# Split weights in seven one-operand tiles and raw weights in four buffers, in a fused convolution and attention layer

## The chip, the cores and the metric

The kernel runs on one core of a Trainium2 chip, in one launch. The metric is the device time of one execution in microseconds, taken as the median of several executions. A core has TensorE (PE in the profile, with its weight loads on a row of their own, PEld), VectorE (DVE), ScalarE (ACT), GpSimd (POOL) and SyncE (SP), which here issues nearly all loads. Each of them works through its instructions in the order that they have in the program.

## The reference

One layer over 512 latent tokens and 256 context tokens of width 1024, in float32. A combined projection `h @ w_in` (1024 x 10240) feeds a gated short convolution and a neighbourhood attention of 16 heads; the two are merged under sigmoid gates and go through a last projection `w_o`.

```python
parts = _split_in(h @ w_in[i])            # b, c, x, z_a, q, k, v, z_b, g_a, g_b, 1024 columns each
q = _apply_rope(_heads(parts[4]), cos, sin)
k = _apply_rope(_heads(parts[5]), cos, sin)
v = _heads(parts[6])
kv_c = hc @ w_in[i][:, K_OFF:V_END]       # keys and values of the context tokens
...
attn = _neighbourhood_attention(q, k, v, k_c, v_c, rpb[i])
y_a = (jax.nn.silu(z_a) * b_gate * _dwconv3(c_gate * x_in, conv_w, conv_b)) @ w_out_conv
y_b = (jax.nn.silu(z_b) * attn_o) @ w_out_attn
merged = jax.nn.sigmoid(g_a) * y_a + jax.nn.sigmoid(g_b) * y_b
y = merged @ w_o
x = x + gt[:, None, :] * _rmsnorm(y, post_g[i])
```

## The kernel before

**Numbers in two parts.** Every large product is done in a reduced-width float32 with each operand cut into a high part H and a low part L. `split` makes them: ACT casts the source to H (L67), then DVE subtracts H from the source and writes L (L70). A product is three matmuls (H·H, H·L, L·H). Weights are split on the fly, and so are the attention's probabilities, whose parts are called TH and TL.

**Chunks.** Weights come in chunks of 256 columns, 1 MB each, in an order that is a list in the program (L237 to L240). A chunk is two raw halves of 512 KB (tile `raw`, L87: three buffers, loaded by SP at L89), each with 512 of the 1024 rows. Split weights live in tiles `w` (L81: four buffers of 8 KB per partition). There are two kinds of chunk:

- An ordinary chunk (`Chunk.split`, L91) takes two `w` tiles, one per half, each with H and L of four row blocks. Two units of 24 matmuls use it (L164 to L166; value chunks go by L177 and L182).
- A paired chunk goes by a Strassen-like scheme with seven products of 12 matmuls (`pair`, L294, the matmuls at L289). `first` (L98) makes four operands, B11 and B21 in one `w` tile, the sums T1 and T2 in another. `second` (L114) makes T3 and T4 in a third and B22 (with B12 where the context needs it) in a fourth. ACT copies results from PSUM (L300 to L311) and DVE adds the others (L306, L314, L317). L306 reads a PSUM bank that the first product of the second half writes again, so that product waits for L306.

The calls of paired and ordinary chunks are interleaved with the attention of earlier heads: scores (PE L717 and L726, DVE L733, ACT L740, L744, L747), `turn2`, which transposes probabilities (PE L754) and splits them into TH and TL, and `gather` (PE L773), which multiplies them with V. After a gather, ACT copies (L778) and DVE adds and gates the result (L779, L780, L785, L786). All these share the instruction streams of ACT and DVE with the splits of the next chunk. Where each stands in its stream is settled when the program is built, by a scheduler that lays out instructions by its own estimates and by when buffers come free. SP's stream holds the raw loads and, between them, the bias loads `bt` (L709) and modulation weights `wm` (L369, L569).

**The end.** The last projection is again a Strassen scheme, on 512-column operands that `moving` (L931) splits: wB11, wB21, wT1, wT2, wT3, wT4, each in two `w` tiles.

Of the kernel before, what the change touches and what calls it, by code (L numbers as in the profile page):

```python
# [15 lines left out]
P = 128  # L16
# [11 lines left out]
def layer(ctx: ExitStack, tc, xp, ctxt, ctxT, cc, wmod, small, wfirst, win, wout, wo, rel, tab, out):  # L28
# [49 lines left out]


    def wtile(shape):  # L80
        return wp.tile(shape, F32R, name="w", bufs=4)  # L81

    class Chunk:


        def __init__(self, src):
            self.raws = [wp.tile([P, 4, 256], F32, name="raw", bufs=3) for _ in range(2)]  # L87
            for i, raw in enumerate(self.raws):
                nc.sync.dma_start(raw, src[:, 4 * i:4 * i + 4])  # L89

        def split(self):  # L91
            t = [wtile([P, 4, 2, 256]) for _ in range(2)]
            for x, raw in zip(t, self.raws):
                split(x[:, :, 0], x[:, :, 1], raw)
            k = range(KT)
            return tuple([t[i // 4][:, i % 4, y] for i in k] for y in range(2)) + ([t[i // 4][:, i % 4] for i in k],)

        def first(self, keep=False):  # L98
            (b11, b12), (b21, b22) = self.b = [(r[:, :, :P], r[:, :, P:]) for r in self.raws]
            t, sums = (wtile([P, 2, 2, 4, P]) for _ in range(2))  # L100
            split(t[:, 0, 0], t[:, 0, 1], b11)
            nc.vector.tensor_add(b11, b11, b12)
            split(sums[:, 0, 0], sums[:, 0, 1], b11)
            split(t[:, 1, 0], t[:, 1, 1], b21)
            nc.vector.tensor_add(b11, b11, b22)
            split(sums[:, 1, 0], sums[:, 1, 1], b11)
            self.keep = keep
            if not keep:
                nc.vector.tensor_add(b12, b12, b22)
            nc.vector.tensor_add(b21, b21, b11)  # L110
            self.B = {"B11": t[:, 0], "B21": t[:, 1], "T1": sums[:, 0], "T2": sums[:, 1]}
            return self

        def second(self):  # L114
            t, last = (wtile([P, 2, 2, 4, P]) for _ in range(2))
            (_, b12), (b21, b22) = self.b
            if self.keep:
                split(last[:, 1, 0], last[:, 1, 1], b12)
                nc.vector.tensor_add(b12, b12, b22)
            for n, x, b in (("T3", t[:, 0], b12), ("T4", t[:, 1], b21), ("B22", last[:, 0], b22)):  # L120
                split(x[:, 0], x[:, 1], b)
                self.B[n] = x
            self.B["B12"] = last[:, 1]


    behind = None
# [1 line left out]
    class Chunks:  # L128
# [13 lines left out]
        def ready(self, n):  # L142
            if n in self.raw:
                c, kind = self.raw.pop(n), self.srcs[n][1]
                self.ahead[n] = c.first(kind == "qk") if kind else c.split()

        def __call__(self):
            self.load(self.n)
# [82 lines left out]
        "cx": lambda j: win[2 * j], "bz": lambda j: win[2 * j + 1],  # L231
    }
    def paired(n, i):
        return n == "g" or n == "qk" and i in (3, 4, 6) or n == "zb" and i < 3 or n in ("cx", "bz") and i > 4

    order = [(win[i], False) for i in range(8)] + [(qk(0), False), (vz(0, 0), False)]
    order += [(where[n](i), n if paired(n, i) else False) for f in plan for n, i in f] + [(vz(3, 1), paired("zb", 3))]  # L237
    merge = ["g2", "g3", "y0", "g4", "y1", "g5", "y2", "g6", "y3", "g7", "y4", "y5", "y6", "y7"]
    order += [(win[32 + int(m[1])], paired("g", int(m[1]))) if m[0] == "g" else (wout[int(m[1])], False) for m in merge]
# [688 lines left out]
        for q in range(2):  # L928
            nc.vector.tensor_add(dst[q], x[q], y[q])

    def moving(src, dst=None):  # L931
        if dst is None:
            t = [wtile([P, 2, 2, S]) for _ in range(2)]
            dst = [[x[:, y] for x in t] for y in range(2)]
        for q in range(2):
            split(dst[0][q], dst[1][q], src[q])
        return dst
# [11 lines left out]
    for j in range(KT):  # L949
        w = chunk()  # L950
        g = [G[j][:, i] for i in range(2)]
        if j in (4, 6):
            raws[j // 2] = G[j]
        m2 = raws[j // 2][:, j % 2]
        for i in range(2):
            nc.vector.scalar_tensor_tensor(
                out=g[i], in0=g[i], scalar=1.0, in1=unit(w, i, ua[i]), op0=ALU.add, op1=ALU.mult
            )
            if j == 7 and i == 0:
                A2 = [bp.tile([P, 2, S], F32R, name=f"A2{k}", tag=f"us{k}") for k in range(4)]  # L960
                for k in range(3):
                    split(A2[k][:, 0], A2[k][:, 1], raws[2 + k // 2][:, k % 2])
        nc.vector.tensor_add(m2, g[0], g[1])
        if j < 4:
            for _ in merge_gates(j + 4):
                pass
        if j == 4:

            nc.vector.tensor_scalar(out=gains[:, 0:4], in0=gains[:, 0:4], scalar1=0.5, scalar2=None, op0=ALU.mult)
            nc.vector.tensor_scalar(out=gains[:, 4:8], in0=gains[:, 4:8], scalar1=-0.5, scalar2=None, op0=ALU.mult)  # L970
            gpost = bp.tile([P, D], F32, name="gpost")
            for i in range(2):
                gb = cv.tile([P, S], F32, name="ta")
                ps = pj()
                for k in range(4):
                    n = 4 * i + k
                    nc.vector.tensor_copy(gb[:, k * P:(k + 1) * P], gains[:, n:n + 1].broadcast_to([P, P]))
                    nc.tensor.transpose(ps[:, k * P:(k + 1) * P], gb[:, k * P:(k + 1) * P], ident)
                nc.scalar.copy(gpost[:, i * S:(i + 1) * S], ps)
        if j == 4:  # L980
            A11, S3 = operand("A11", hp, ("u2", "u3")), operand("S3", hp, ("a2", "a3"))
            for q in range(2):
                split(A11[q][:, 0], A11[q][:, 1], raws[q][:, :, h0])
                x = cv.tile([P, S], F32, name="tb").rearrange("p (k c) -> p k c", k=2)
                nc.vector.tensor_sub(x, raws[q][:, :, h0], raws[q][:, :, h1])
                split(S3[q][:, 0], S3[q][:, 1], x)
            B11, B12 = quarter("B11", hp, ("s0", "s1")), quarter("B12", hp, ("u0", "u1"))
            B22, B21, T2, T3 = (quarter(n, hp, (f"h{2 * i}", f"h{2 * i + 1}")) for i, n in enumerate(("B22", "B21", "T2", "T3")))
            for t, i in ((B11, (0, 0)), (B12, (0, 1)), (B22, (1, 1)), (B21, (1, 0))):
                load_block(t, *i)  # L990
        if j == 5:
            sums1(0)
        if j == 6:
            nc.scalar.activation(const.tile([P, 1], F32, name="dummy2"), G[7][:, 1, :1], AF.Sqrt, bias=eps, scale=0.0)
            wB11 = moving(B11)
            total(B11, B11, B12)
            T1 = B11
            total(T2, T1, B22)
            total(T3, B12, B22)
            T4 = B12  # L1000
            total(T4, T2, B21)
# [63 lines left out]
    sums1(1)  # L1065
    for q in range(2):
        split(X1[q][:, 0], X1[q][:, 1], raws[q][:, :, h1])
    wT1 = moving(T1)
    both(fb, a12, wB21, True)
    for q in range(2):  # L1070
        split(S2[q][:, 0], S2[q][:, 1], raws[q][:, :, h0])
# [12 lines left out]
        squares(t, c0, 0, added(P1s[:, t], fb[t]))  # L1084
        partial(t, 0, True)
    both(fa, stationary(S2), wT2, False, snap(U2s, fa))
    wT3 = moving(T3)

    def block12(t):
        squares(t, c1, 1, added(U2s[:, t], fe[t]))  # L1090
# [113 lines left out]
```

## Time and profile before

| | |
|---|---|
| median of 3 runs | 709.25 us (709.1 to 709.57) |
| profiled execution | 709.01 us, its span 707.2 us |
| busy | PE 695.0 us (98%), DVE 586.3 (83%), ACT 436.5 (62%), POOL 66.9 (9%) |
| chain that ended last | PE 91%, DVE 4%, DMA 2%, ACT 1% |
| TensorE clock granted | 1.00 in every stage |

The span is the time from the first to the last instruction in the profile; 1.8 us of the execution's time lie outside it. A row of the timeline gives start, duration, engine, line, operation, output and inputs, and how many like instructions it merges; in brackets stands how long the engine was idle before it, and what ended the wait. Durations on ACT and DVE overlap a little, so that the distance between two starts is shorter than a duration.

### The profile page before, as it was taken

The page shows a single profiled execution, that of the slowest core. Times are in us where ns is not written, and L with a number is a line of the kernel's source. Part 1 is how long each engine was busy: PE and PEld are TensorE (multiplying, and loading weights), DVE is VectorE, ACT ScalarE, POOL GpSimd, SP SyncE. Part 2 cuts the span into 40 slices and gives each one's busy share as a digit, 9 for nine tenths or more (in the row PEclk, how much of TensorE's full clock was granted, in tenths as well). Part 3 has the DMA queues.
Part 4 walks back from the last instruction along what each step waited for, and adds up shares of the span by engine and source line. Part 5 has one row for each costly group of instructions (what it writes and reads, how often), then busy time and mean ns, then how long its engine had stood idle before and what let it go on. Part 6 is the DMA issues. An engine that isn't in the chain of part 4 may idle for free.

```text
span 707.2 us, 11426 instructions
## 1 busy us (share of the span) xinstructions
PE 695.0 (98%) x4196; PEld 618.0 (87%) x4196; DVE 586.3 (83%) x1114; ACT 436.5 (62%) x868; POOL 66.9 (9%) x110
## 2 busy tenths in 40 slices
PE   7999999999999999999999999999999999999996
PEld 4888888888889989898999999999898899988885
DVE  6979997668599989978898797999799676665996
ACT  6566632656577677775876766778693444442563
POOL 0000002230130310301302203000000000000000
PEclk9999999999999999999999999999999999999998
DMA  8996896564351563542635436313733233560013
GB/s 338 406 354 227 284 339 173 131 164 144 99 105 24 135 176 116 127 138 60 168 106 165 103 125 157 101 61 105 247 117 116 87 120 120 198 250 30 31 59 120
DMA packets 37466, 108.27 MB, mean 153 GB/s; under 512 B 5025, under 2 KB 5281, under 8 KB 37410
## 3 DMA queue, kind: packets, MB, share of 16 engines
q1 hardware_dynamic: 28946, 92.20, 37.8%
q0 software_dynamic: 8320, 15.21, 10.7%
q8 instruction: 33, 0.54, 0.3%
q14 instruction: 23, 0.19, 0.1%
q10 hardware_dynamic: 144, 0.13, 0.1%
HBM read 87.07 MB, written 5.24 MB: 131 GB/s over the span
## 4 chain that ended last, share of the span: by engine, by line
PE 91%; DVE 4%; DMA 2%; ACT 1%; issue 1%; SPq 0%; POOL 0%; DVEq 0%; ACTq 0%
PE ps L289 25%; PE ps L164 11%; PE ps L166 11%; PE ps L165 11%; PE ps L177 6%; PE ps L1008 5%; PE ps L773 4%; PE ps L754 3%; PE ps L182 3%; PE ps L717 3%; PE ps L196 2%; PE ps L424 2%; PE ps L428 2%; PE ps L425 2%; DMA fraw<-in_wfirst 1%; PE ps L726 1%
## 5 line engine op out<-in xcount | busy, mean ns | idle before, releaser
L67 ACT CAST w<-raw 128x512 fp32r<-128x512 f32 (+1 forms) x193 | 137.3, 733 | 95.9 <-PE ps L166 31.3
L70 DVE TENSOR_TENSOR w<-raw,w 128x512 fp32r<-128x512 f32 (+1 forms) x193 | 156.6, 824 | 42.3 <-ACT w L67 40.9
L289 PE MATMUL ps<-S,w 128*128 128x256 f32 x960 | 121.9, 283 | 0.0
L289 PEld LDWEIGHTS ps<-S,w 128*128 128x128 f32 x960 | 118.2, 192 | 0.1
L289 PE MATMUL ps<-h,w 128*128 128x256 f32 x720 | 94.0, 284 | 0.6 <-DVE tc L306 0.5
L289 PEld LDWEIGHTS ps<-h,w 128*128 128x128 f32 x720 | 89.9, 191 | 2.5 <-DVE tc L306 0.7
L164 PE MATMUL ps<-h,w 128*128 128x512 f32 x208 | 81.5, 392 | 0.0
L166 PE MATMUL ps<-h,w 128*128 128x512 f32 x208 | 81.2, 390 | 0.0
L165 PE MATMUL ps<-h,w 128*128 128x512 f32 x208 | 81.0, 390 | 0.0
L626 POOL DMA_DIRECT2D tc<-tb x32 | 28.8, 1175 | 286.7 <-DVE tc L624 197.7
L747 ACT ACTIVATE pt<-pt,z 128x512 f32<-128x512 f32 x64 | 43.0, 724 | 6.0 <-DVE z L745 5.9
L166 PEld LDWEIGHTS ps<-h,w 128*128 128x128 f32 x208 | 39.0, 188 | 8.3
L165 PEld LDWEIGHTS ps<-h,w 128*128 128x128 f32 x208 | 39.1, 188 | 8.0
L164 PEld LDWEIGHTS ps<-h,w 128*128 128x128 f32 x208 | 39.1, 188 | 7.9
L67 ACT CAST TH<-ps 128x512 fp32r<-128x512 f32 x64 | 35.8, 589 | 15.5 <-PE ps L754 15.5
L733 DVE CUSTOM_DVE_ANT_1 ps<-ps,bt 128x512 f32<-128x512 f32 x56 | 38.8, 693 | 6.8 <-PE ps L717 6.5
L70 DVE TENSOR_TENSOR TL<-ps,TH 128x512 fp32r<-128x512 f32 x64 | 42.2, 682 | 1.0 <-ACT TH L67 0.7
L754 PE MATMUL ps<-ident,pt 128*128 128x128 f32 x256 | 33.3, 273 | 0.0
L177 PE MATMUL ps<-w,h 128*128 128x512 f32 x128 | 32.3, 394 | 0.0
L754 PEld LDWEIGHTS ps<-ident,pt 128*128 128x128 f32 x256 | 29.2, 140 | 2.1 <-ACT pt L747 0.2
L740 ACT ACTIVATE pt<-ps,m 128x512 f32<-128x512 f32 x32 | 22.0, 688 | 12.5 <-DVE m L733 11.8
L773 PE MATMUL ps<-TH,V 128*128 128x256 f32 (+1 forms) x96 | 28.5, 319 | 0.2 <-ACT TH L67 0.2
(249 smaller groups left out, 1387.8 us busy)
## 6 DMA issues: line engine op xcount, KB each, us to landing
raw<-in_win SPq DMA_DIRECT2D x74, 512.0 KB, 4.4
wm<-in_wmod SPq DMA_DIRECT2D x34, 512.0 KB, 6.4
raw<-in_wout SPq DMA_DIRECT2D x16, 512.0 KB, 3.6
bt<-in_rel SPq DMA_DIRECT2D x16, 256.0 KB, 2.9
tc<-tb POOLq DMA_DIRECT2D x32, 128.0 KB, 3.6
B<-in_wo SPq DMA_DIRECT2D x8, 512.0 KB, 6.4
fraw<-in_wfirst SPq DMA_DIRECT2D x8, 384.0 KB, 8.6
qd<-qd POOLq DMA_DIRECT2D x24, 128.0 KB, 2.3
```

Source lines behind the costliest of these rows:

```text
L67: cast = nc.scalar.copy(H, src)
L70: nc.vector.tensor_sub(L, src, H.bitcast(F32))
L164: nc.tensor.matmul(ps, lhsT=H[k][:, cs], rhs=mH[k], start=k == 0, stop=False)
L165: nc.tensor.matmul(ps, lhsT=H[k][:, cs], rhs=mL[k], start=False, stop=False)
L166: nc.tensor.matmul(ps, lhsT=L[k][:, cs], rhs=mH[k], start=False, stop=k == KT - 1)
L177: nc.tensor.matmul(ps, lhsT=mH[k][:, ts], rhs=both[k].rearrange("p a c -> p (a c)"), start=k == 0, stop=False, skip_group_check=True,)
L289: nc.tensor.matmul(ps, lhsT=w[:, x, k], rhs=act[y][k], start=start and k + o == 0, stop=k == 3 and o == 2, skip_group_check=True,)
L733: nc.vector.tensor_tensor_reduce(out=s3, in0=s3, in1=bt[:, e::4 - e][:, 0:2], scale=-1.0, scalar=3.0e38, op0=ALU.add, op1=ALU.min, accum_o ...
L747: nc.scalar.mul(x, x, z[:, i:i + 1])
L754: nc.tensor.transpose(tp[:, c], pt[:, c * P:(c + 1) * P], ident)
L773: nc.tensor.matmul(o3[:, dst], lhsT=V[p][:, kt, h], rhs=src(t), start=n == 0 and t is TH, stop=n == len(work) - 1 and t is TL,)
L1008: nc.tensor.matmul(out, lhsT=a(x, k, ts), rhs=w[y][k // 2][:, k % 2, cols], start=start and k + o == 0, stop=k == 3 and o == 2, skip_group ...
```

## The change

The raw weights get a fourth buffer, so two whole chunks fit. The split weights get seven tiles of 4 KB per partition, one operand each: one of the Strassen operands (H and L side by side), or H alone or L alone of half an ordinary chunk. The four value chunks, whose matmuls want H and L side by side, take four tiles with a quarter of the chunk's rows each (`beside`), so they are split in four pairs of 128x512 instructions and not in two of 128x1024. The value chunks are marked "v" in the list for that, and `ready` sends them to `split`. In the last projection wB11, wT1 and wT3 go into the four raw buffers (`spare`), the others into four `w` tiles. Together both pools hold as much as before: 4·8 + 3·4 = 44 KB per partition, and now 7·4 + 4·4 = 44 KB. No matmul is added or removed. Below line 125 a line of the changed kernel has a number higher by 7 (10 from L940 on) than before.

```diff
     def wtile(shape):
-        return wp.tile(shape, F32R, name="w", bufs=4)
+        return wp.tile(shape, F32R, name="w", bufs=7)
...
-            self.raws = [wp.tile([P, 4, 256], F32, name="raw", bufs=3) for _ in range(2)]
+            self.raws = [wp.tile([P, 4, 256], F32, name="raw", bufs=4) for _ in range(2)]
...
-        def split(self):
-            t = [wtile([P, 4, 2, 256]) for _ in range(2)]
-            for x, raw in zip(t, self.raws):
-                split(x[:, :, 0], x[:, :, 1], raw)
+        def split(self, beside=False):
+
             k = range(KT)
-            return tuple([t[i // 4][:, i % 4, y] for i in k] for y in range(2)) + ([t[i // 4][:, i % 4] for i in k],)
+            if beside:
+                t = [wtile([P, 2, 2, 256]) for _ in range(4)]
+                for i, x in enumerate(t):
+                    split(x[:, :, 0], x[:, :, 1], self.raws[i // 2][:, 2 * (i % 2):2 * (i % 2) + 2])
+                return tuple([t[i // 2][:, i % 2, y] for i in k] for y in range(2)) + ([t[i // 2][:, i % 2] for i in k],)
+            t = []
+            for raw in self.raws:
+                t.append([wtile([P, 4, 256]) for _ in range(2)])
+                split(*t[-1], raw)
+            return tuple([t[i // 4][y][:, i % 4] for i in k] for y in range(2)) + (None,)
+
+        def operand(self, name, b):
+            x = self.B[name] = wtile([P, 2, 4, P])
+            split(x[:, 0], x[:, 1], b)
 
         def first(self, keep=False):
...
-            t, sums = (wtile([P, 2, 2, 4, P]) for _ in range(2))
-            split(t[:, 0, 0], t[:, 0, 1], b11)
+            self.B = {}
+            self.operand("B11", b11)
             nc.vector.tensor_add(b11, b11, b12)
-            split(sums[:, 0, 0], sums[:, 0, 1], b11)
-            split(t[:, 1, 0], t[:, 1, 1], b21)
+            self.operand("T1", b11)
+            self.operand("B21", b21)
             nc.vector.tensor_add(b11, b11, b22)
-            split(sums[:, 1, 0], sums[:, 1, 1], b11)
+            self.operand("T2", b11)
...
         def second(self):
...
-            for n, x, b in (("T3", t[:, 0], b12), ("T4", t[:, 1], b21), ("B22", last[:, 0], b22)):
-                split(x[:, 0], x[:, 1], b)
-                self.B[n] = x
+            for n, b in (("T3", b12), ("T4", b21), ("B22", b22)):
+                self.operand(n, b)
...
-                self.ahead[n] = c.first(kind == "qk") if kind else c.split()
+                self.ahead[n] = c.first(kind == "qk") if kind and kind != "v" else c.split(kind == "v")
...
-    def moving(src, dst=None):
+    def moving(src, dst=None, spare=False):
         if dst is None:
-            t = [wtile([P, 2, 2, S]) for _ in range(2)]
-            dst = [[x[:, y] for x in t] for y in range(2)]
+            if spare:
+                t = [wp.tile([P, 2, S], F32R, name="wr", tag="raw", bufs=4) for _ in range(4)]
+            else:
+                t = [wtile([P, 2, S]) for _ in range(4)]
+            dst = t[::2], t[1::2]
...
-            wB11 = moving(B11)
+            wB11 = moving(B11, spare=True)
...
-    wT1 = moving(T1)
+    wT1 = moving(T1, spare=True)
...
-    wT3 = moving(T3)
+    wT3 = moving(T3, spare=True)
```

The change also moves instructions. Three places are shown, of the kernel before and then of the changed one. The paired chunk in them is the convolution's chunk cx 5; its raw halves are raw_2547 and raw_2548 before and raw_2586 and raw_2587 after.

SP's loads up to that chunk and the next, before:

```order
L89 DMA raw_2313<-in_win 128x1024
L709 DMA bt_1039<-in_rel 128x512 x2
L89 DMA raw_2314<-in_win 128x1024
L89 DMA raw_2547<-in_win 128x1024
L709 DMA bt_1039<-in_rel 128x512
L89 DMA raw_2548<-in_win 128x1024
L89 DMA raw_2736<-in_win 128x1024
```

and in the change:

```order
L89 DMA raw_2349<-in_win 128x1024
L283 DMA usc4_98<-ta_1743 128x512
L716 DMA bt_1051<-in_rel 128x512
L89 DMA raw_2350<-in_win 128x1024
L716 DMA bt_1051<-in_rel 128x512
L89 DMA raw_2586<-in_win 128x1024
L89 DMA raw_2587<-in_win 128x1024
L716 DMA bt_1051<-in_rel 128x512
L89 DMA raw_2778<-in_win 128x1024
```

The two halves of the chunk now stand next to each other, ahead of the bias load that stood between them. Before, the second half goes into the buffer of raw_2313, the first half of the chunk just ahead of it; now it goes into that of raw_2004, the last half of the chunk before that one.

ACT's stream around the gather that comes next, before (L67 with TH is the split of transposed probabilities, L303, L305 copies of results, L744 an exponential):

```order
L67 CAST w_2575<-raw_2547 128x512
L303 COPY tc_2483<-ps_2494 128x256
L305 COPY tc_2483<-ps_2492 128x256
L67 CAST w_2575<-raw_2548 128x512
L67 CAST TH_2342<-ps_2561 128x512
L744 ACTIVATE pt_2556,z_2470<-ps_2551,m_2554 128x512
L67 CAST TH_2342<-ps_2562 128x512
L67 CAST w_2576<-raw_2547 128x512
```

and in the change:

```order
L310 COPY tc_2521<-ps_2533 128x256
L312 COPY tc_2521<-ps_2531 128x256
L67 CAST TH_2378<-ps_2600 128x512
L67 CAST TH_2378<-ps_2601 128x512
L751 ACTIVATE pt_2595,z_2508<-ps_2590,m_2593 128x512
L754 ACTIVATE pt_2507<-pt_2507,z_2508 128x512
L754 ACTIVATE pt_2595<-pt_2595,z_2508 128x512
L67 CAST w_2618<-raw_2586 128x512
L67 CAST w_2621<-raw_2587 128x512
```

The cast from the chunk's second raw half (raw_2548, raw_2587) stood ahead of both TH casts and stands behind them now, and so do the subtractions that follow on DVE.

DVE's stream ahead of the add L306 of that chunk (L313 in the change), before (tb and at are the gate and the attention's result, kl a key's low part, L733 the score's bias and minimum):

```order
L779 TENSOR_TENSOR at2_2643<-ps_2644,ta_2657 64x448
L785 SCALAR_TENSOR_TENSOR tb_2629<-tb_2629,tc_2482 128x512
L785 SCALAR_TENSOR_TENSOR tb_2633<-tb_2633,tc_2483 128x512
L786 SCALAR_TENSOR_TENSOR at0_1589<-at0_1589,tb_2629 128x512
L786 SCALAR_TENSOR_TENSOR at0_1589<-at0_1589,tb_2633 128x512
L70 TENSOR_TENSOR kl_2440<-tc_2257,ks_2438 128x512
L780 TENSOR_TENSOR at2_2643<-ps_2644,ta_2657 64x64
L733 ISA ps_2661,m_2664<-ps_2661,bt_1039 128x512
L733 ISA m_2664 128x1
L70 TENSOR_TENSOR w_2673<-raw_2548,w_2673 128x512
L70 TENSOR_TENSOR w_2674<-raw_2548,w_2674 128x512
L306 TENSOR_TENSOR tc_2671<-tc_2671,ps_2682 128x256
```

and in the change:

```order
L787 TENSOR_TENSOR at2_2684<-ps_2685,ta_2698 64x64
L740 ISA ps_2702,m_2705<-ps_2702,bt_1051 128x512
L740 ISA m_2705 128x1
L792 SCALAR_TENSOR_TENSOR tb_2670<-tb_2670,tc_2520 128x512
L792 SCALAR_TENSOR_TENSOR tb_2674<-tb_2674,tc_2521 128x512
L793 SCALAR_TENSOR_TENSOR at0_1613<-at0_1613,tb_2670 128x512
L793 SCALAR_TENSOR_TENSOR at0_1613<-at0_1613,tb_2674 128x512
L70 TENSOR_TENSOR kl_2478<-tc_2293,ks_2476 128x512
L70 TENSOR_TENSOR w_2714<-raw_2586,w_2714 128x512
L70 TENSOR_TENSOR w_2717<-raw_2587,w_2717 128x512
L70 TENSOR_TENSOR w_2720<-raw_2587,w_2720 128x512
L313 TENSOR_TENSOR tc_2712<-tc_2712,ps_2724 128x256
```

All three subtractions of the chunk's second half now stand between the gate and the add, where two of them stood before (the first, from raw_2547, stood ahead of L779).

More of the change, by code (lines that the diff above doesn't have):

```diff
@@ L110, in first @@
             nc.vector.tensor_add(b21, b21, b11)
-            self.B = {"B11": t[:, 0], "B21": t[:, 1], "T1": sums[:, 0], "T2": sums[:, 1]}
             return self
         def second(self):
-            t, last = (wtile([P, 2, 2, 4, P]) for _ in range(2))
             (_, b12), (b21, b22) = self.b
             if self.keep:
-                split(last[:, 1, 0], last[:, 1, 1], b12)
+                self.operand("B12", b12)
                 nc.vector.tensor_add(b12, b12, b22)
-            for n, x, b in (("T3", t[:, 0], b12), ("T4", t[:, 1], b21), ("B22", last[:, 0], b22)):
-                split(x[:, 0], x[:, 1], b)
-                self.B[n] = x
-            self.B["B12"] = last[:, 1]
+            for n, b in (("T3", b12), ("T4", b21), ("B22", b22)):
+                self.operand(n, b)
     behind = None
@@ L233, in paired @@
     def paired(n, i):
-        return n == "g" or n == "qk" and i in (3, 4, 6) or n == "zb" and i < 3 or n in ("cx", "bz") and i > 4
-    order = [(win[i], False) for i in range(8)] + [(qk(0), False), (vz(0, 0), False)]
+        return n == "v" or n == "g" or n == "qk" and i in (3, 4, 6) or n == "zb" and i < 3 or n in ("cx", "bz") and i > 4
+    order = [(win[i], False) for i in range(8)] + [(qk(0), False), (vz(0, 0), "v")]
     order += [(where[n](i), n if paired(n, i) else False) for f in plan for n, i in f] + [(vz(3, 1), paired("zb", 3))]
```

## The prediction

> **What bounds the kernel now.** I read the shares of the page first, then the chain of waits.
>
> ```profile
> PE 695.0 (98%) x4196; PEld 618.0 (87%) x4196; DVE 586.3 (83%) x1114; ACT 436.5 (62%) x868; POOL 66.9 (9%) x110
> PE 91%; DVE 4%; DMA 2%; ACT 1%; issue 1%; SPq 0%; POOL 0%; DVEq 0%; ACTq 0%
> ```
>
> TensorE is the bound, and no matmul changes. The change can give no more than the time in which TensorE stands still behind a split, a load or something queued behind these. The busy time by stretches of 20 us (columns: PE, PEld, DVE, ACT, POOL, each with its count, then clock, DMA share, GB/s) is 20.00 for PE in all stretches from 20 to 700 us but two:
>
> ```profile
> 220.00:240.00 20.00, 20.00 (x149) 18.93 (x148) 18.88 (x43) 16.04 (x38) 0.00 (x0) 1.00 0.19 56
> 240.00:260.00 20.00, 19.38 (x151) 18.43 (x150) 17.52 (x37) 14.77 (x32) 7.20 (x11) 1.00 0.61 152
> 260.00:280.00 20.00, 19.44 (x153) 18.51 (x152) 19.03 (x41) 14.89 (x33) 1.03 (x2) 1.00 0.41 133
> ```
>
> The waits of TensorE name who ended them (us in total, times, longest); the others lie in the first 20 us, before any chunk:
>
> ```profile
> PE ps L289 <- DVE tc L306: 0.5, 1, 0.5
> PE ps L773 <- DVE TL L70: 0.5, 1, 0.5
> PE ps L773 <- ACT TH L67: 0.2, 1, 0.2
> ```
>
> A busy row of PE overlaps the next one, so a stall costs more than the idle time shown. I take it from distances between starts on PE's timeline:
>
> ```profile
> 247.04 1.04 PE L754 MATMUL ps<-ident,pt 128*128 128x128 f32 x8
> 247.84 1.68 PE L289 MATMUL ps<-h,w 128*128 128x256 f32 x12
> 249.35 3.04 PE L289 MATMUL ps<-S,w 128*128 128x256 f32 x24
> 252.55 0.49 PE L773 MATMUL ps<-TH,V 128*128 128x512 f32 x1 [0.16 <-ACT TH L67]
> 253.50 0.50 PE L773 MATMUL ps<-TL,V 128*128 128x512 f32 x1 [0.45 <-DVE TL L70]
> 253.83 0.40 PE L773 MATMUL ps<-TH,V 128*128 128x512 f32 x1
> 254.07 0.39 PE L773 MATMUL ps<-TL,V 128*128 128x512 f32 x1
> ...
> 261.93 1.03 PE L754 MATMUL ps<-ident,pt 128*128 128x128 f32 x8
> 263.44 1.69 PE L289 MATMUL ps<-h,w 128*128 128x256 f32 x12 [0.47 <-DVE tc L306]
> ...
> 269.57 3.46 PE L289 MATMUL ps<-h,w 128*128 128x256 f32 x24
> ```
>
> *First stall, the gather at 252.55.* The 24 matmuls ahead of it stand 0.12 apart and should hand over at 249.35 + 24·0.12 = 252.23: 0.32 us late. From its TH to its TL go 0.95 us where the next pair needs 0.24 (253.83 to 254.07): 0.71. The next start is another 0.09 late. Together 1.12. *Second, the product at 263.44.* Eight transposes take 0.80 us up to the next start at 247.04, and 1.51 at 261.93: 0.71. *Third, inside 269.57.* 24 matmuls take 3.46 where those at 249.35 take 3.04; 0.08 of the 0.42 is the usual slow first one (1.68 for the 12 at 247.84, which at 0.12 would make 1.60), so 0.34. Sum: 2.17 us. That is the whole prize between 20 and 700 us.
>
> Why is the first gather late? Its splits stand behind the chunk's second raw half, on ACT and on DVE, and that half came late:
>
> ```profile
> 228.50 0.89 SPq L89 DMA_DIRECT2D raw<-in_win  x2
> 238.58 0.33 SPq L709 DMA_DIRECT2D bt<-in_rel  x1
> 244.39 2.38 SPq L89 DMA_DIRECT2D raw<-in_win  x2
> ```
>
> ```profile
> 250.24 0.62 ACT L67 CAST w<-raw 128x512 fp32r<-128x512 f32 x1 [3.08 <-DMA raw<-in_win]
> 250.76 0.58 ACT L67 CAST TH<-ps 128x512 fp32r<-128x512 f32 x1
> 251.91 0.59 ACT L67 CAST TH<-ps 128x512 fp32r<-128x512 f32 x1
> ```
>
> ```profile
> 243.64 1.29 DVE L70 TENSOR_TENSOR w<-raw,w 128x512 fp32r<-128x512 f32 x2
> 250.89 0.69 DVE L70 TENSOR_TENSOR w<-raw,w 128x512 fp32r<-128x512 f32 x1 [2.19 <-ACT w L67]
> ...
> 258.02 1.28 DVE L785 SCALAR_TENSOR_TENSOR tb<-tb,tc 128x512 f32<-128x512 f32 x2
> 259.23 1.28 DVE L786 SCALAR_TENSOR_TENSOR at<-at,tb 128x512 f32<-128x512 f32 x2
> 260.43 0.68 DVE L70 TENSOR_TENSOR kl<-tc,ks 128x512 fp32r<-128x512 f32 x1
> 261.77 1.28 DVE L70 TENSOR_TENSOR w<-raw,w 128x512 fp32r<-128x512 f32 x2
> 262.98 0.41 DVE L306 TENSOR_TENSOR tc<-tc,ps 128x256 f32<-128x256 f32 x1
> 270.86 0.41 DVE L317 TENSOR_TENSOR tc<-tc,ps 128x256 f32<-128x256 f32 x1
> ```
>
> With three raw buffers the half raw_2548 has to wait for the last split from raw_2313, done at about 244.3; it is issued at 244.39, and ACT waits 3.08 us for it with both TH casts queued behind.
>
> **The change part by part.** *Fourth raw buffer.* By the order shown, raw_2587 goes into the buffer of raw_2004, a value chunk's half, and stands behind no bias load any more. The pair at 228.50 shows when SP is free for it, and that chunk has been split by then; so it lands some 15 us earlier, into a stretch whose DMA share is 0.19. The bias load that was issued at 238.58 now stands behind it and is not held up. The scheduler has also put both TH casts ahead of that half's split. From the first TH cast to the end of TL there are four instructions on two engines and no wait for a load; the transposes they read end by 248.1 (247.04 + 1.04), so with DVE's distances of 0.60 (1.29 less 0.69 in the row of 243.64) TL is done at about 249.6, 2.6 us ahead of the 252.23 at which it is wanted. First stall: -1.12. If the load were late after all: 0.
>
> *Second stall, same price.* The product waits for L306, which waits for DVE's own stream: 258.02 to 263.39 is unbroken work of 0.60 a piece. In the changed order three, not two, subtractions of the chunk stand between gate and add (+0.60), but the work ahead of the gate starts earlier, as DVE no longer idles 2.19 us. What decides is when the gate can start: the gather's result is ready 1.12 earlier, ACT copies it behind two more casts, and I put L779 at about 255.5. Then follow L779 and L780 (0.67), L733 (0.60), four gate instructions (2.40), kl (0.60), three subtractions (1.80), L306 (0.41): 262.0, and 0.25 for small gaps, 262.25. TensorE wants it at 261.93 + 0.80 - 1.12 = 261.61. So about 0.64 us of the 0.71 stays. Bounds: 0 if L306 profits by the 2.19 us in full; 1.23 if DVE moves up only with the gather (263.39 - 1.12 + 0.60 against 261.61).
>
> *Third stall.* L317 at 270.86 ends 0.34 too late for its product, with a queue of sums and splits of the next chunk ahead. Its splits no longer share a tile, so they are spread; I walk B21 of that chunk to 268.3, wanted at 269.8, and take -0.34. Bounds: 0 and -0.34.
>
> *Seven one-operand tiles.* A tile comes free with its one operand, so splits of the next paired chunk can begin piece by piece. Ordinary chunks get less: two of them used all four tiles, and now the eighth piece, L of the second half, must wait until the first piece of the chunk before is read out. This shows in waits that are there already:
>
> ```profile
> ACT w L67 <- PE ps L166: 44.6, 20, 7.1
> ```
>
> ```profile
> 85.66 0.39 PE L165 MATMUL ps<-h,w 128*128 128x512 f32 x1
> ...
> 98.35 0.39 PE L164 MATMUL ps<-h,w 128*128 128x512 f32 x1
> ```
>
> Such a chunk runs 2·24 matmuls, 0.2266 apart (56 steps from the first row to the last), 10.9 us. Its first piece is last read after 36 of them, at 8.2; the next chunk's eighth piece is wanted at its fifth row block, 10.9 + 12·0.2266 = 13.6. That leaves 5.4 us for one subtraction of 1.2. No cost taken; the bounds are in the third rival.
>
> *Value chunks in quarters.* Eight casts and eight subtractions more. By the rows
>
> ```profile
> 254.39 1.16 ACT L67 CAST w<-raw 128x512 fp32r<-128x512 f32 x2
> 44.74 2.00 ACT L67 CAST w<-raw 128x1024 fp32r<-128x1024 f32 x2
> 45.83 2.36 DVE L70 TENSOR_TENSOR w<-raw,w 128x1024 fp32r<-128x1024 f32 x2 [0.27 <-ACT w L67]
> ```
>
> and the one at 243.64, starts stand 0.52 and 0.96 apart on ACT (1.16 - 0.64, 2.00 - 1.04), 0.60 and 1.14 on DVE (2.36 - 1.22). Two halves cost 0.08 more on ACT and 0.06 more on DVE than one whole: 0.64 and 0.48 us in all, over four places with slack. Nothing on the path; all of it if that slack were gone: +0.5. The Trainium skill, Perfetto Trace Analysis, section Optimizing Scalar/DVE Operations, gives about 93 ns and 60 ns of overhead per instruction on SBUF; an estimate from that page is 0.74 and 0.48, and the trace's 80 and 60 ns agree.
>
> *The end.* wB11, wT1 and wT3 use raw buffers. TensorE's stretches up to 700 us are full and stay so; the tail behind the last matmul is untouched: 0.
>
> *Reordering elsewhere.* DVE's and ACT's streams change in many places, and some products start within tenths of what they wait for:
>
> ```profile
> 486.35 0.67 DVE L70 TENSOR_TENSOR TL<-ps,TH 128x512 fp32r<-128x512 f32 x1
> 487.13 0.45 PE L773 MATMUL ps<-TL,V 128*128 128x512 f32 x1
> ```
>
> Here 0.11 us are left. In the change one more instruction (0.60) stands ahead of this TL, but four matmuls of the next half (0.48) have moved ahead of the gather on PE. One slip of this kind costs up to 0.6; bounds 0 to 1.2, I take 0.2.
>
> Sum: -1.12 - 0.07 - 0.34 + 0.2 = -1.3 us. Against the profiled execution of 709.01 (span 707.2, 1.8 around it) that is 707.7; the median stands 0.24 higher, so **707.9**.
>
> **The rivals.** *All of it comes back* (L306 profits in full, no slips): 709.25 - 2.17 = 707.1. For it: 2.19 us of DVE idle are regained just ahead. Against: 19.03 of 20 us busy in that stretch.
>
> *DVE is the real limit there, and the stall moves on.* The first stall goes, the second grows to 1.23, the third stays, slips cost 0.2 to 0.6: -1.12 + 0.52 + 0.2 to 0.6 = -0.4 to 0, about 709.0. For it: DVE's 19.03, and the extra subtraction ahead of L306. Against: the regained idle time. [...]
>
> *Slower: the eighth piece at the head of the queue.* ACT and DVE take their streams in order. A split that waits for TensorE to free one of seven tiles blocks the TH, TL or L733 behind it. Seven ordinary chunks run among attention work. It decides once the blocked split is more than 5.4 - 1.2 = 4.2 us late, or stands ahead of a TL with tenths to spare. Each stall then costs what the first one here costs, 1.12; from three on the gain of 1.3 is lost and 709.25 - 1.3 + 3·1.12 = 711.3. For it: waits for L166 up to 7.1 us already. Against: the 4.2 us.
>
> *It doesn't do what it says:* raw_2587 is still held on SP, behind a bias load. Then all three stalls stay: 709.2. Against: the order shown.
>
> **How the numbers follow.** Forecast 0.42, its own range 707.3 to 708.6; all back 0.13; stall moves on 0.25; not earlier 0.06; slower 0.14. What a measurement of this kernel can tell from no change is 0.2%, 1.4 us: below 707.83 is faster. All back and nearly half of the forecast lie there with a little of the rest, so faster 0.36; slower 0.14 is the third rival; same 0.50. The range leaves out part of the first and of the slower rival: 706.9 to 710.6.
>
> **What would show it.** The wait for TL and TH at L780 gone from TensorE's list, PE 20.00 in 240 to 260, and the cast from the second raw half without a wait for DMA. A wait for L313 (the former L306) of 0.4 to 0.6 remaining at about 262. Raw loads in pairs at about 228.5. It is wrong if new waits appear for w, TL or TH elsewhere, if the wait for L313 grows past 1 us, or if the matmuls' own distances change.

## The result and the profile after

The changed kernel takes 712.51 us (median of 8 runs, 709.89 to 714.35) against 709.26 (709.03 to 709.57): a ratio of 1.005, with a 95% interval of 1.0038 to 1.0062. It is slower, and its runs lie 4.5 us apart where those of before, on the same chip, lie 0.5 apart (in later comparisons 0.9 to 1.9). The first profile was of its quickest execution, 709.89 us (span 708.1). I took a second, of an execution of 712.38 us (span 710.6), and the text below goes by that one unless it says otherwise.

The page's shares and chain, second profile:

```profile
PE 696.4 (98%) x4196; PEld 618.8 (87%) x4196; DVE 585.7 (82%) x1122; ACT 434.4 (61%) x876; POOL 66.9 (9%) x110
PE 86%; DVE 6%; DMA 3%; ACT 2%; issue 1%; SPq 1%; POOL 0%; DVEq 0%; ACTq 0%
```

The work is the same to about 2 us on every engine. The chain has lost 5 points of PE to DVE, DMA and ACT: TensorE waits more. Its stretches of 20 us in the second profile (columns as before) show where:

```profile
160.00:180.00 20.00, 19.98 (x102) 16.72 (x100) 19.16 (x38) 14.21 (x28) 2.06 (x4) 1.00 0.42 116
200.00:220.00 20.00, 18.85 (x112) 16.30 (x111) 16.53 (x41) 12.40 (x32) 3.51 (x7) 1.00 0.49 105
240.00:260.00 20.00, 19.14 (x141) 17.71 (x140) 18.62 (x41) 14.82 (x33) 6.69 (x10) 1.00 0.57 130
260.00:280.00 20.00, 18.48 (x147) 17.72 (x146) 17.81 (x39) 14.09 (x33) 1.54 (x3) 1.00 0.42 124
```

The stretch from 200 to 220 us, full before, has lost 1.15 us of PE and some 3 us of DVE (19.62 before). The list of TensorE's waits names new ones, and the wait for L306 (L313 in the change) is no longer among those of 0.2 us and more:

```profile
PE ps L724 <- DMA ks<-kl: 1.4, 1, 1.4
PE ps L780 <- ACT TH L67: 0.7, 1, 0.7
PE ps L296 <- DVE ta L215: 0.6, 1, 0.6
PE ps L780 <- DVE TL L70: 0.4, 1, 0.4
PE ps L296 <- DVE tc L324: 0.2, 1, 0.2
```

L780 is the gather, but not the one near 252 us that held TensorE before. That one (at 254.20 in the first profile of the change) runs without a gap:

```profile
254.20 0.40 PE L780 MATMUL ps<-TH,V 128*128 128x512 f32 x1
254.44 0.40 PE L780 MATMUL ps<-TL,V 128*128 128x512 f32 x1
```

The stalls of the second profile are these, on PE's timeline:

```profile
208.40 0.50 PE L780 MATMUL ps<-TH,V 128*128 128x512 f32 x1 [0.72 <-ACT TH L67]
209.33 0.50 PE L780 MATMUL ps<-TL,V 128*128 128x512 f32 x1 [0.43 <-DVE TL L70]
...
246.55 1.69 PE L296 MATMUL ps<-S,w 128*128 128x256 f32 x12 [0.58 <-DVE ta L215]
...
271.64 0.50 PE L724 MATMUL ps<-ks,qd 128*128 128x512 f32 x1 [1.40 <-DMA ks<-kl]
```

Measured as in the prediction, by the distance between two starts less the regular one, and leaving out those under 0.11 us and one of 0.20 near 68 us that every kernel has, they add up as follows (us; the later columns are the experiments below). By this measure the prediction's three stalls come to 1.93 us and not 2.17; the third is 0.25.

| place | before | change, 1st | change, 2nd | hold_only | pin2 | pin2_hold |
|---|---|---|---|---|---|---|
| gather near 167 | 0 | 0 | 0.17 | 0.65 | 0 | 0 |
| gather near 208 | 0 | 0.70 | 1.58 | 1.98 | 0 | 0 |
| 245 to 264 | 1.68 | 1.49 | 1.63 | 1.50 | 0.28 | 0.29 |
| 266 to 272 | 0.25 | 0.44 | 1.56 | 0.15 | 1.57 | 0.26 |
| profiled execution | 709.01 | 709.89 | 712.38 | 711.70 | 708.68 | 707.41 |

Before and second profile differ by 3.01 us in these rows and by 3.37 in time. The place that grew most is one that the prediction had passed over.

**The gather near 208 us.** ACT's timeline before, with the two TH casts at 202.96 and 204.67 and the cast of the keys `ks<-tc` behind them:

```profile
202.96 0.58 ACT L67 CAST TH<-ps 128x512 fp32r<-128x512 f32 x1
...
204.67 0.58 ACT L67 CAST TH<-ps 128x512 fp32r<-128x512 f32 x1
...
205.40 0.65 ACT L67 CAST ks<-tc 128x512 fp32r<-128x512 f32 x1
```

In the second profile of the change:

```profile
205.11 0.62 ACT L67 CAST ks<-tc 128x512 fp32r<-128x512 f32 x1 [3.57 <-DMA tc<-tb]
205.63 0.58 ACT L67 CAST TH<-ps 128x512 fp32r<-128x512 f32 x1
...
207.75 0.59 ACT L67 CAST TH<-ps 128x512 fp32r<-128x512 f32 x1
```

The keys' cast has been moved ahead of both TH casts. It waits for the rotary step's transfer `tc<-tb`, which GpSimd issues (its last issue ends at 199.87), and ACT stands still for 3.57 us with TH, and so TL, queued behind. In the first profile of the change the same wait is shorter:

```profile
203.91 0.62 ACT L67 CAST ks<-tc 128x512 fp32r<-128x512 f32 x1 [2.79 <-DMA tc<-tb]
```

How late the gather is now depends on how long a transfer takes in that execution. Before, no product of TensorE hung on it.

The transfer is also slower than before. From 195 to 207 us SP issued only a bias load before; in the second profile of the change a raw load follows it while the rotary transfers are under way:

```profile
200.27 0.33 SPq L89 DMA_DIRECT2D raw<-in_win  x1
```

The rotary transfers in the issues' view of 195 to 208 us (KB each, median us to landing), before and then in the second profile:

```profile
tc<-tb POOLq DMA_DIRECT2D x2, 128.0 KB, 4.3
tc<-tb POOLq DMA_DIRECT2D x2, 128.0 KB, 5.1
```

In eight_raw3, an experiment below without such a load there, they take 4.3 again. No run moves this load alone, so it is not shown that the load is the cause.

The gather near 167 us goes the same way, with the keys of head pair 1. Where their cast waits 2.41 us for its transfer (pin2) the gather has no stall; with 2.96 (second profile) it has 0.17 us, with 3.44 (hold_only) 0.65 and with 3.64 (pin2_early3) 0.85. Before, the cast waited 0.77.

**The score near 270 us.** The key's low part kl goes to another tile by two transfers `ks<-kl`, and the score L724 waits for them. Its stall varies from 0.44 to 1.56 us between the two profiles, although its instructions stand in the same order. Which of the two, order or transfer, costs what, is a question for experiments.

### The profile page after: what moved, and what is told of

It is laid out like the page before. It is cut to its first block, busy times and chain, and to the rows that moved or that the text cites. A ratio compares the mean times of both kernels' runs of the same rounds, so it can differ in the third digit from the quotient of the medians.

```text
span 708.1 us, 11428 instructions
## 1 busy us (share of the span) xinstructions
PE 695.8 (98%) x4196; PEld 618.4 (87%) x4196; DVE 585.4 (83%) x1122; ACT 434.4 (61%) x876; POOL 66.8 (9%) x110
## 3 DMA queue, kind: packets, MB, share of 16 engines
HBM read 87.07 MB, written 5.24 MB: 130 GB/s over the span
## 4 chain that ended last, share of the span: by engine, by line
PE 86%; DVE 6%; DMA 3%; ACT 2%; issue 1%; SPq 0%; POOL 0%; DVEq 0%; ACTq 0%
PE ps L296 24%; PE ps L172 11%; PE ps L171 11%; PE ps L173 11%; PE ps L1018 5%; PE ps L184 5%; PE ps L780 3%; PE ps L761 3%; PE ps L724 3%; PE ps L189 2%; PE ps L431 2%; PE ps L435 2%; PE ps L432 2%; PE ps L203 2%; DVE w L70 1%; DMA tc<-tb 1%
## 5 line engine op out<-in xcount | busy, mean ns | idle before, releaser
L67 ACT CAST w<-raw 128x512 fp32r<-128x512 f32 (+1 forms) x201 | 137.6, 711 | 87.0 <-PE ps L172 25.6
L67 ACT CAST TH<-ps 128x512 fp32r<-128x512 f32 x64 | 36.0, 588 | 17.0 <-PE ps L761 16.9
L780 PE MATMUL ps<-TH,V 128*128 128x256 f32 (+1 forms) x96 | 28.5, 319 | 0.0
```

Source lines behind the costliest of these rows:

```text
L67: cast = nc.scalar.copy(H, src)
L780: nc.tensor.matmul(o3[:, dst], lhsT=V[p][:, kt, h], rhs=src(t), start=n == 0 and t is TH, stop=n == len(work) - 1 and t is TL,)
```

## The experiments

Two theories of the loss were set against each other at first: that the *order* of ACT's and DVE's streams costs the time, through instructions that wait for a transfer ahead of others that TensorE needs; and that the *buffers* do, through waits for w tiles or raw halves.

### Again, one pin, other tiles

`again` is the changed kernel itself.

> The changed kernel once more, for a profile of a run nearer to its median of 712.5 us (the first profile was of its quickest run, 709.9). Order theory: the extra time of a usual run lies in few places where ACT or DVE has an instruction that waits for a transfer issued by GpSimd (tc<-tb of the rotary step, ks<-kl) ahead of one that TensorE needs; at the gather near 207 us TensorE loses 1 to 4 us, not the 0.8 of the quick run. Buffer theory: the extra time lies in waits for w tiles or raw halves. Contention theory: matmuls or loads everywhere are a little slower and no single place holds more than 1 us.

Measured: 711.39 us (5 runs, 710.71 to 712.38), ratio 1.0034 (1.0021 to 1.0047). The stalls are those above: two places hold most of them, both behind transfers, and ACT's waits for raw halves have shrunk. Before:

```profile
ACT w L67 <- DMA raw<-in_win: 24.1, 18, 4.1
```

and in this profile:

```profile
ACT w L67 <- DMA raw<-in_win: 4.7, 1, 4.7
```

So the buffers do what they are for; TensorE had not been waiting there.

`pin` fixes the keys' cast in program order for all head pairs. (`blocks` is true for paired chunks, whose cast is fixed in both kernels.)

```diff
-            keys(k, slice(0, S), blocks)
+            keys(k, slice(0, S), True)
```

> The changed kernel, but the cast of the keys that waits for the rotary transfer keeps its place in the program for all head pairs, not only for those of paired chunks; in the build it moves behind both TH casts of the gather near 207 us. Buffers as changed. Order theory: the stall at that gather goes, the time comes to 708.5 to 710.5 us and the spread shrinks. Buffer theory: still 712 to 713.

Measured: 710.90 us (8 runs, 710.13 to 712.93), ratio 1.0031 (1.002 to 1.0042). The stalls at 208 to 260 are gone, but the pin also moves the cast of the first head pair's keys, from 125.04 in the second profile of the change to 139.70; the score near 148 us then waits for their transfer, a new stall of 1.97 us, and that near 270 stays (1.77). The order theory's place was right, its time (708.5 to 710.5) was not: one pin too many.

`eight_raw3` has eight one-operand tiles and three raw buffers; `seven_raw3`, run later, has seven and three. In both the last projection uses w tiles (`spare` taken out).

```diff
-        return wp.tile(shape, F32R, name="w", bufs=7)
+        return wp.tile(shape, F32R, name="w", bufs=8)
-            self.raws = [wp.tile([P, 4, 256], F32, name="raw", bufs=4) for _ in range(2)]
+            self.raws = [wp.tile([P, 4, 256], F32, name="raw", bufs=3) for _ in range(2)]
-            wB11 = moving(B11, spare=True)
+            wB11 = moving(B11)
```

> One-operand tiles alone: eight of them (as many bytes as the four of before), raw weights in three buffers as before, the last projection in w tiles. Order theory: again another order, so any time from 708.5 to 713, by what stands ahead of TH and TL at the gathers; the wait for the second raw half at 250 us returns (1 us). Buffer theory, where seven tiles are one too few: 709 or less.

Measured: 713.77 us (4 runs, 712.59 to 714.61), ratio 1.0066 (1.0051 to 1.0081). Here the gather near 208 is not held up, but the next one is (TH and TL near 230, 1.43 us), and the score near 270 again (1.25).

> Seven one-operand tiles with three raw buffers, the last projection in w tiles: the fourth raw buffer undone. Theory that the fourth buffer makes loads collide with the key transfers: the stall near 270 us falls below 0.5 us and the wait for the second raw half (1 us, near 252) returns. Theory that only the order counts: stalls at other places, 709 to 714, and the key transfer still late.

Measured: 714.16 us (4 runs, 711.27 to 715.25), ratio 1.007 (1.0051 to 1.0089). The stalls near 167 (0.77), 208 (1.25), 246 and 271 (1.64) are those of the changed kernel. Two parts of my expectation fell: the wait at the gather near 252 did not come back with three buffers, and the score's stall did not need the fourth. One-operand tiles alone bring both the gain and the losses.

`nospare` leaves the raw buffers out of the last projection.

> The changed kernel with wB11, wT1 and wT3 in w tiles and not in the raw buffers. Order theory: nothing before 640 us changes, so within 1 us of the changed kernel (712 to 713), unless the wait for w tiles in the last projection shows on TensorE. If the end costs time in the changed kernel: below 711.5.

Measured: 712.54 us (4 runs, 711.88 to 713.92), ratio 1.0052 (1.0037 to 1.0067): no difference from the changed kernel, as expected. The end plays no part.

### One cast moved back

`pin2` pins the keys' cast of head pair 2 alone:

```diff
-            keys(k, slice(0, S), blocks)
+            keys(k, slice(0, S), blocks or p == 2)
```

> The changed kernel with one cast pinned: that of the keys of head pair 2 keeps its place in the program. The build differs from the changed kernel in 8 rows on ACT and 12 on DVE around the gather near 208 us and in none on TensorE and SP. Order theory: the stalls at 208 (1.6 us in the second profile) and those that follow from it go; the wait for the keys' transfer near 270 us (0.4 to 1.7) stays, so 709.5 to 711 us. Buffer theory: no change, 711.4 to 712.5.

Measured: 708.68 us (11 runs, 707.99 to 711.42), ratio to before 0.9999 (0.999 to 1.0008). Ten instructions of DVE and ACT in another place (each shows twice in the 20 rows) return some 3 us, with all buffers as in the change. The keys' cast is behind the TH casts; the first starts 0.16 us after its transpose and the gather is on time. With it go the stalls near 246, 251 and 260 us, forty microseconds later. What connects them is DVE: in the changed kernel it stood idle for TH,

```profile
205.05 0.69 DVE L70 TENSOR_TENSOR TL<-ps,TH 128x512 fp32r<-128x512 f32 x1 [2.41 <-ACT TH L67]
```

(first profile), in a part of the program where it is almost full (19.62 us of 20 in the stretch from 200 us before, 18.88 in the next), and carried the delay along. The add L215 (L208 before) frees a PSUM bank for the product wanted at 243.70 before. It starts at

```profile
242.09 0.41 DVE L208 TENSOR_TENSOR ta<-ta,ps 128x256 f32<-128x256 f32 x1
```

before, at

```profile
246.08 0.41 DVE L215 TENSOR_TENSOR ta<-ta,ps 128x256 f32<-128x256 f32 x1
```

in the second profile of the change, and at

```profile
242.95 0.41 DVE L215 TENSOR_TENSOR ta<-ta,ps 128x256 f32<-128x256 f32 x1
```

in pin2. One stall is left in pin2, of 1.57 us, at the score.

### The keys' transfer

Two ways to explain that last stall: kl is subtracted too late (lateness), or the transfers take too long beside other traffic (contention). GpSimd's and SP's issues in pin2:

```profile
260.46 0.51 POOL L698 DMA_DIRECT2D ks<-kl  x1 [1.59 <-DVE kl L70]
261.23 0.52 POOL L699 DMA_DIRECT2D ks<-kl  x1 [0.26 <-DMA ks<-ks]
```

```profile
259.59 0.33 SPq L809 DMA_DIRECT2D asc<-at  x1
260.83 1.64 SPq L89 DMA_DIRECT2D raw<-in_win  x2
262.99 0.33 SPq L716 DMA_DIRECT2D bt<-in_rel  x1
```

A store of 512 KB and two raw halves of 512 KB go out within 3 us of the key transfers. Before, one raw half went out near them, at 263.12, behind the same store at 260.53.

`pin2_early3` takes the keys of head pair 3 one step earlier:

```diff
-        later.append((rest, 2 if blocks else 1))
+        later.append((rest, 2 if blocks and p != 3 else 1))
```

> As pin2, and the keys of head pair 3 are cut into parts one step earlier in the program, so that DVE subtracts kl ahead of the gate and not behind it (row 409 and not 432), and GpSimd issues the two key transfers some 10 us earlier, away from the two raw loads and the store at 262 to 265 us. Order theory: the stall near 270 us goes too, 707.5 to 709. If the loads in pairs slow everything (contention theory): the stall moves to another transfer and the time stays within 0.5 us of pin2.

Measured: 709.90 us (11 runs, 709.1 to 711.42), ratio 1.0015 (1.0006 to 1.0024). The score's stall is gone, but the keys' cast now stands ahead of both TH casts, where it waits 3.25 us for the rotary transfer, and kl stands ahead of TL. The gather near 254 us waits 1.33 us, the next products 0.51 and 1.36. Neither theory had this; it is the mechanism of the gather near 208 us again. Another 0.85 us of this profile lie at the gather near 167 us, which this edit does not touch.

`pin2_un3` frees that cast instead:

```diff
-            keys(k, slice(0, S), blocks or p == 2)
+            keys(k, slice(0, S), blocks and p != 3 or p == 2)
```

> As pin2, but the cast of the keys of head pair 3 is free to move; DVE's kl then stands behind the gather's TL and ahead of the gate (row 413, not 430 as before), ACT's cast ahead of both TH casts, where it waits for the rotary transfer. Lateness theory: kl is ready about 8 us earlier, the stall near 268 us goes, 707.0 to 707.8, if TH is not held up; if the rotary transfer lands after 250 us, TL comes late at the gather near 252 us, as in the kernel before, 708 to 709.5.

Measured: 710.99 us (6 runs, 710.62 to 711.57), ratio 1.0028 (1.0016 to 1.0039). The score's stall is gone and a larger one has come. ACT:

```profile
251.46 0.62 ACT L67 CAST ks<-tc 128x512 fp32r<-128x512 f32 x1 [4.57 <-DMA tc<-tb]
251.98 0.37 ACT L310 COPY tc<-ps 128x256 f32<-128x256 f32 x1
252.24 0.38 ACT L312 COPY tc<-ps 128x256 f32<-128x256 f32 x1
```

and TensorE:

```profile
252.67 1.65 PE L296 MATMUL ps<-S,w 128*128 128x256 f32 x6 [2.23 <-ACT tc L312]
```

The transfer landed only after 251 us. Not TH suffered first, as I had written, but two short copies of PSUM behind the cast. In this profile too the gather near 167 us, outside the edit, loses 0.75 us.

`pin2_hold` leaves all instructions of TensorE, DVE and ACT where they are in pin2 and holds back the two stores of attention results on SP until after the next bias load (`last` is that load; the expectation names only the first store):

```diff
+                last[:] = [nc.sync.dma_start(bt[:, 2 * h:2 * h + 2], rel[p, h])]
...
-            nc.sync.dma_start(asc[g], attn[2 * g, "both"])
+            t = attn[2 * g, "both"]
+            def store():
+                with tc.issue_after(last[0].ins):
+                    nc.sync.dma_start(asc[g], t)
+            later.append((store, 6))
```

> As pin2, with one store (the first attention result, 512 KB) held on SP until after the next bias load; the streams of TensorE, DVE and ACT are the same row for row. In pin2 that store goes out at 259.6 and two raw loads from 260.8, while GpSimd's two key transfers go out at 260.5 and 261.2. Contention theory: the key transfers land sooner, the stall near 268 us falls from 1.4 to 0.8 or less, time 707.6 to 708.3. Lateness theory (the transfers only start too late): stall and time as in pin2, 708.5 to 708.9.

Measured: 707.41 us (11 runs, 706.97 to 708.16), ratio to before 0.9979 (0.997 to 0.9988): faster than both kernels. The key transfers are issued at 260.53 and 261.23 and the raw loads from 260.91, all to within 0.1 us of pin2; the store goes out at 263.45 and not at 259.59. The issues' view (from 256 to 270 us) has for pin2

```profile
raw<-in_win SPq DMA_DIRECT2D x2, 512.0 KB, 6.6
ks<-kl POOLq DMA_DIRECT2D x2, 192.0 KB, 5.7
```

and for pin2_hold

```profile
raw<-in_win SPq DMA_DIRECT2D x2, 512.0 KB, 5.5
ks<-kl POOLq DMA_DIRECT2D x2, 192.0 KB, 4.4
```

The score follows, pin2 first, then pin2_hold:

```profile
267.95 0.50 PE L724 MATMUL ps<-ks,qd 128*128 128x512 f32 x1 [1.41 <-DMA ks<-kl]
```

```profile
266.71 0.50 PE L724 MATMUL ps<-ks,qd 128*128 128x512 f32 x1
```

1.3 us off the transfers, 1.31 us off the stall (1.57 to 0.26), 1.27 us off the time. Contention it is, for this amount; the lateness theory had forecast no change.

`hold_only` has the held stores and not the pin; `before_hold` has them in the kernel before. In both, TensorE, DVE and ACT stand row for row as in their base.

> The changed kernel with the held stores (both, of the first and of the second attention result) and without the pinned cast: TensorE, DVE and ACT stand row for row as in the changed kernel. If the two causes add up: the stall near 270 us falls by about 1.2, those at 208 to 263 us stay, so the changed kernel's 711.4 to 712.5 less 1.2, 710.2 to 711.3. If the collision is the whole loss: 709 or less.

Measured: 711.13 us (10 runs, 709.26 to 711.72), ratio 1.0024 (1.0014 to 1.0033). Within the range of adding up, at its upper end: the stall near 270 fell to 0.15, while those near 167 and 208 were longer in that profile (0.65 and 1.98).

> The kernel before with the same held stores, all other streams row for row as before. Before has no stall at the score near 268 us, so by the order and contention theories nothing changes: 708.8 to 709.4, ratio within 0.1% of 1. If the held stores are of use by themselves, it would gain as much as pin2 gained by them, 1.2 us.

Measured: 709.00 us (11 runs, 708.16 to 709.53), ratio 0.9995 (0.9987 to 1.0004). No change, as expected: in the kernel before, the store's place costs nothing.

### What the fourth raw buffer is worth

`fixed_raw3` is pin2_hold with three raw buffers and the last projection in w tiles.

> Seven tiles, three raw buffers (and so wB11, wT1 and wT3 in w tiles), with both repairs of pin2_hold, the pinned cast and the held stores. Prediction's own theory, that the fourth raw buffer is what removes the wait before the first gather: that wait (1.1 us near 252) is back, 708.5 or more. Order theory, by which TH and TL now stand ahead of the second raw half whether it is early or late: no stall at that gather; any difference from pin2_hold (707.4) comes from the other rows that the scheduler moved, about 120 of them on TensorE, within 1 us.

Measured: 709.13 us (12 runs, 707.31 to 710.22), ratio 0.9999 (0.9991 to 1.0008). The second raw half is issued late again,

```profile
244.50 2.89 SPq L89 DMA_DIRECT2D raw<-in_win  x2
```

yet TH is cast at once,

```profile
247.50 1.08 ACT L67 CAST TH<-ps 128x512 fp32r<-128x512 f32 x2 [0.38 <-PE ps L761]
251.08 1.12 ACT L67 CAST w<-raw 128x512 fp32r<-128x512 f32 x2
```

and the gather has no stall. So the early load is not needed: with TH ahead of the split the stall is gone even when the half comes late. Whether an early load alone, in the old order, would remove it was not tried. The fourth buffer, with the spare use in the last projection that came with it, is worth 1.7 us all the same (709.13 against 707.41, with the rows that the scheduler moved along), in part at a place I had not looked at. In the profile with three, casts from raw halves stand ahead of the copy L307 near 527 us, and one of them waits for its load:

```profile
521.66 0.62 ACT L67 CAST w<-raw 128x512 fp32r<-128x512 f32 x1 [1.33 <-DMA raw<-in_win]
...
527.13 0.35 ACT L307 COPY g<-ps 128x256 f32<-128x256 f32 x1
```

TensorE loses 0.83 us there and none with four. The two profiled executions differ by 0.78 us (708.19 and 707.41), so between them this is nearly all; the profiled execution of fixed_raw3 was quicker than its median by 0.94, and what the others lose is not accounted for. From 460 to 540 us, counting stalls over 0.11 us, TensorE loses 1.47 us in eight_raw3, 0.68 in seven_raw3 and 1.00 in fixed_raw3, each with three buffers and small tiles; before and in every kernel with four raw buffers it loses nothing there. That the load is what delays the copy was read from the rows and not tried by itself.

## Why the prediction was wrong, point by point

Forecast: 707.9 us, range 706.9 to 710.6. Measured: 712.51, outside it and on the other side of 709.25.

- *What bounds the kernel, and the prize of 2.17 us:* right. TensorE's stalls decided, and with the two repairs the time came to 1.6 us below before, 707.41.
- *First stall, -1.12:* right in size, wrong in its condition. The gather near 252 is on time in the change, with four raw buffers and with three. I named both the earlier load and the new place of TH, but let the gain hang on the load (0 if it were late). It did come earlier (233.11 in the first profile, 244.39 before), but fixed_raw3 shows that the order alone is enough.
- *Second stall, 0.64 of it stays:* DVE's part was right, and TensorE's order was overlooked. In pin2 L313 ends at 262.30, where I had 262.25:

```profile
261.89 0.41 DVE L313 TENSOR_TENSOR tc<-tc,ps 128x256 f32<-128x256 f32 x1
```

  Yet no wait for it is left on TensorE, because the scheduler moved six matmuls of another product in between:

```profile
261.20 1.03 PE L761 MATMUL ps<-ident,pt 128*128 128x128 f32 x8
261.99 0.96 PE L296 MATMUL ps<-S,w 128*128 128x256 f32 x6
262.78 1.60 PE L296 MATMUL ps<-h,w 128*128 128x256 f32 x12
```

  Before, the product followed the transposes at once; in that order it would have been wanted at 262.00, some 0.3 us too early, and now it is wanted at 262.78. So this term came out well by a move that I had not seen. Another 0.28 us go to the copy L307, which ends at 259.12 in pin2. (My upper bound, 1.23, comes to 1.26 by its own terms.)
- *Third stall, -0.34:* right; it is gone in pin2, in pin2_hold and in the change as it stands. By the table's measure it was worth 0.25.
- *Seven tiles, the eighth piece, no cost:* no list of TensorE's waits, in any of the runs, names a w tile. The third rival came near the time (711.3) by luck: what stood at the head of ACT's queue was not a split waiting for a tile, but the keys' cast waiting for a transfer.
- *Value chunks in quarters, the end:* no cost found. nospare is the same, and ACT's and DVE's busy times did not rise. The quarters were not tried by themselves.
- *Reordering elsewhere, 0.2 (0 to 1.2):* this is the step that failed. I had bounded one slip by the length of one instruction, 0.6 us. A slip behind an instruction that waits for a transfer costs what is left of the transfer's delay, 0.70, 1.58 and 1.98 us near 208 where ACT's wait was 2.79, 3.57 and 3.98, and then DVE carries it to the stalls near 246 to 263, since it had too little slack there to make it up. By pin2 (708.68) against the change (711.39 and 712.51) the one misplaced cast, with the instructions that its pin moves, costs 2.7 to 3.8 us.
- *The fourth buffer's loads land in a quiet stretch:* true of the chunk that I looked at, whose pair goes out at 231.91 in the first profile, and not of the next loads, which go out as a pair at 260 to 265 us beside a store and the key transfers. The term missing from the sum is the score near 268: 1.3 us by pin2_hold against pin2. seven_raw3 shows that three raw buffers don't prevent it; what frees the buffers together are the one-operand tiles.

With these, the sum reads: the design's gain of about 1.6 us, less 1.3 for the transfers' collision, less 2.7 to 3.8 for the cast: 2.4 to 3.5 us slower. Measured: 3.3 and 2.3. (Gain, collision and cast are differences of the same runs; the independent test of their adding up is hold_only.)

## What to carry to other kernels

When a change lets a scheduler reorder, list in each in-order stream the instructions that wait for a transfer, and see what stands behind each of them that the bounding engine needs: their price is what is left of the transfer's delay, not an instruction's length, and on a nearly full engine it reappears far down the stream. Earlier or bunched loads must be laid against every transfer in the same few microseconds on which a product waits; holding back a store that nobody waits for can be enough. A wider spread between executions is a reason to look at transfers: here it grew from 0.5 to 4.5 us, and the stalls that varied were those behind a transfer.

## What the runs showed of the hardware

Traffic on SP's queue slowed GpSimd's transfers: with one 512 KB store issued 3.9 us later, at unchanged issue times, two transfers of 192 KB landed in 4.4 and not 5.7 us, and the two raw halves beside them in 5.5 and not 6.6. In the second profile of the change the same key transfers took 5.7, and before 4.4.

The time of the rotary transfer also changes from execution to execution. The end of GpSimd's two issues and the start of ACT's cast, in the first profile of the change,

```profile
197.59 1.86 POOL L633 DMA_DIRECT2D tc<-tb  x2
```

lie 4.46 us apart, from 199.45 to 203.91, and in the second

```profile
198.00 1.87 POOL L633 DMA_DIRECT2D tc<-tb  x2
```

5.24, from 199.87 to 205.11. Before, the cast came at 205.40, behind both, and nothing on TensorE followed the difference.
